# Three edits in a fused transformer-layer kernel: decay rows asked for earlier, one product moved from ScalarE to GpSimd, four loads moved to another queue

## The chip, the cores and the metric

One core of a Trainium2 chip runs the whole program. The core has five engines that run side by side, each with an instruction queue of its own that it works through in order: TensorE (PE; weight loads are shown apart as PEld), VectorE (DVE), ScalarE (ACT), GpSimd (POOL) and SyncE (SP), which does no arithmetic and issues transfers. Transfers can be issued from SP's, ACT's and POOL's queues. The metric is the device time of one launch in microseconds (us).

## The reference

One layer of a streaming encoder works on 576 tokens (a prompt of 512 and a second sequence of 64), with 1024 channels in float32:

```python
def layer(x, lp, st):
    h = x + 0.5 * swiglu(rmsnorm(x, lp['norm_ffn1']), lp['w_ffn1_in'], lp['w_ffn1_out'])
    mix, new_st = mixer(rmsnorm(h, lp['norm_mix']), lp, st)
    h = h + mix
    h = h + 0.5 * swiglu(rmsnorm(h, lp['norm_ffn2']), lp['w_ffn2_in'], lp['w_ffn2_out'])
    return h, new_st
```

The mixer projects its input once and feeds three branches: a state-space scan (SSD: 16 heads in 4 groups), attention over a band of chunks (8 heads), and a matrix memory (mLSTM: 4 heads). In the two scans a running sum of decays along the tokens is used three ways:

```python
# SSD, one chunk
cum = jnp.cumsum(dtc * a, axis=1)
seg = cum[:, :, None] - cum[:, None, :]
lmat = jnp.exp(jnp.where(causal, seg, -jnp.inf))
w = cb[..., None] * lmat * dtc[:, None]
y = jnp.einsum('btsgr,bsgrp->btgrp', w, xc)
y = y + jnp.exp(cum)[..., None] * jnp.einsum('btgn,bgrpn->btgrp', cc, h)
last = cum[:, -1]
wd = jnp.exp(last[:, None] - cum) * dtc
h = jnp.exp(last)[..., None, None] * h + jnp.einsum('bsgr,bsgn,bsgrp->bgrpn', wd, bc, xc)
```

The three branches are normed, projected, weighted by gates (a sigmoid of part of the same projection), summed and projected once more.

## The kernel before

Tokens lie along the free dimension in five chunks (`CH`: four of 128 and one of 64), channels on the 128 partitions. A float32 product is made of three TensorE products of rounded parts: each weight block is split into `ph` (a cast on ACT, L288) and `pl` (the difference, on DVE, L289), and so are the inputs. Weights come through rings of buffers: SP's queue loads `wr` and `wx` blocks from DRAM (L237, L460, L467), POOL adds some of them (an accumulating transfer at L461, sums `wy` and `wx` at L472), ACT and DVE make the parts. Large products use seven block products in place of eight (`stream`, `product`, L616); their results lie in PSUM accumulators that ACT (L533, L540) or DVE (L542) must read out before TensorE can fill them again.

In the mixer the projection runs as one long sequence of such block products (`pairs`), and the small work of the branches is threaded into it. Each branch unit is a Python generator: `attn(i)`, `ml(h)`, `ssd(g)`. `product` calls `tick` once, ahead of its twelve matmuls; `tick` advances `side` (the generator `gates`, which makes decay sums from the gate rows at the start of the stage) and the first unit of `jobs`. A `yield n` in a unit means that its next part is emitted n products later. Units are queued in the order `ORDER` (a0 a1 m0 s0 a2 a3 s1 m1 s2 m2 s3 m3), each when its projections have been emitted. What is emitted is then ordered on each engine by a planner that simulates time: it goes by the order of emission, with `high_priority` and `issue_after` to move it, and issues ahead what is ready.

The running sums per head lie as single rows in a DRAM scratch (`scr`, 24 rows: 0 to 15 SSD's, 16 to 19 and 20 to 23 mLSTM's). `gates` writes them with three stores on SP (L839, L853, L856). A unit reads them back spread over 128 partitions: `rows(r0, n, step)` is an access pattern with partition stride 0, one or two rows wide. They land in `R1`, a tile of eight rows of 576 that holds the residual at other times: rows 0 and 1 hold SSD's gate z, rows 2 to 4 and 5 to 7 are two slots, handed out in turn by `b` to each mLSTM unit and each half of an SSD unit (a unit `ssd(g)` has two halves j = 0, 1 of two heads). All these loads are issued from ACT's queue, L181 and L1175, at the start of the unit that uses them.

In `ssd`, per half: from the spread rows come `wd` (DVE L1209, L1210, then ACT L1214) and `el` (ACT L1212, L1213); x is transposed by TensorE, and DVE writes it scaled by dt into `xd` (L1219, L1223). ACT makes `xw` = `xd` x `wd`, one instruction per chunk and head (L1228). The spread rows themselves become the decay matrix in place (ACT L1234 per chunk, L1236, L1237; POOL L1238, L1239). TensorE then makes the state products from `xw` (L1252) and the outputs (L1274, L1281). The result goes by POOL (L1283 to L1287) to the DRAM scratch `ys`.

`attn` loads its bias (ACT's queue, L916) into one of two buffers `bias` and prepares it on POOL (L918 to L921); DVE adds it to the scores (L965, L980, L981).

After the last unit, `merge` reads the branch outputs `ys` back (tile `y`, L1340), splits them into `YH`, `YL`, and multiplies. Its first four loads, attention's, are issued from SP's queue with raised priority, the others and the gates (L1354) from POOL's.

Of the kernel before, what the change touches and what calls it, by code (L numbers as in the profile page):

```python
# [27 lines left out]
AF = mybir.ActivationFunctionType  # L28
ALU = mybir.AluOpType
AX = mybir.AxisListType  # L30

T = 576
TP = 512
HALVES = ((0, 256), (256, 320))
CH = [(0, 128), (128, 128), (256, 128), (384, 128), (512, 64)]
# [1 line left out]
NS = 115  # L37
FH = 288
NPLAIN = 4
BUFS = {"g": 9, "t": 5, "P": 4, "Q": 2, "bias": 2}  # L40

FBUFS = {"P": 5, "g": 5, "s": 3}
WBUFS = {"wr": 5, "wx": 4, "wy": 2, "ph": 6, "pl": 6}
# [38 lines left out]
class Hybrid:  # L82
    def __init__(self, ctx, tc, I, O):
        self.tc, self.nc, self.I, self.O = tc, tc.nc, I, O
        self.op = None
        self.stay = {}
        self.plan = []
        self.splan = []
        self.ahead = {}
        self.pin = {}  # L90
        self.b_i = 0
        self.jobs, self.gap, self.side = deque(), 0, iter(())
        nc = self.nc
        self.const = ctx.enter_context(tc.tile_pool(name="const", bufs=1))
        self.dram = ctx.enter_context(tc.tile_pool(name="scr", bufs=1, space=bass.MemoryType.DRAM))
        c = self.const
        self.R1 = c.tile([128, 8, T], F32, name="R1")
        self.rs = c.tile([128, T], F32, name="rs")
        self.small = ctx.enter_context(tc.tile_pool(name="small", bufs=8, reuse_waits="tile"))

        self.wt = ctx.enter_context(tc.tile_pool(name="wt", bufs=1, reuse_waits="tile"))
        self.xs = self.dram.tile([128, 8, T], F32, name="xs")

        self.ys = [self.dram.tile([128, T], F32, name=f"ys{i}") for i in range(16)]
        self.gs = [self.dram.tile([128, T], F32, name=f"gs{i}") for i in range(24)]
        self.scr = self.dram.tile([24, T], F32, name="scr_rows")
# [55 lines left out]
    def t(self, tag, shape=(128, T)):  # L162
        pool = self.gp if tag == "g" else self.fp
        return pool.tile(list(shape), F32, name=tag, tag=tag, bufs=BUFS[tag])

    def P(self, shape=(128, T)):
        pool, bufs = (self.fp, BUFS["P"]) if self.mixer else (self.wp, FBUFS["P"])
        return pool.tile(list(shape), F32, name="P", tag="P", bufs=bufs)

    def Q(self, shape=(128, 5, 128)):  # L170
        return self.fp.tile(list(shape), F32, name="Q", tag="Q", bufs=BUFS["Q"])

    def unit(self, shape, tag, bufs):
        return self.fp.tile(list(shape), F32, name=tag, tag=tag, bufs=bufs)

    def b(self, step, r0):


        i = 2 + self.b_i % 2 * 3
        self.b_i += 1  # L180
        self.nc.scalar.dma_start(self.R1[:, i:i + 2, :], self.rows(r0, 128, step))  # L181
        return [self.R1[:, i + j, :] for j in range(3)]

    def bank(self):
        i = self.bank_i % self.banks
# [598 lines left out]
    def gates(self, pre):  # L784
# [3 lines left out]
        nc, TM = self.nc, self.TM  # L788
        view = lambda i, w: self.R1[:, i, 0:5 * w].rearrange("p (c w) -> p c w", w=w)
        X, u, d, p, q = view(1, 24), view(2, 20), view(3, 20), view(4, 20), view(5, 20)  # L790
        nc.gpsimd.memset(X[64:128, 4, :], 0.0)
        ps = self.ps("x")
        for c, (a, n) in enumerate(CH):
            nc.tensor.transpose(ps[:n, c * 24:(c + 1) * 24], pre[0:24, a:a + n], self.ident[0:24, 0:24])
# [34 lines left out]
        nc.vector.tensor_tensor(TM[:, :, 64:68], X[:, :, 20:24], TM[:, :, 96:100], op=ALU.subtract)  # L829
        yield  # L830
        RT, b, g, M, ei = (self.R1[:, i, :] for i in (6, 2, 3, 4, 5))
        ps, ps2 = self.ps("x"), self.ps("s")
        for c, (a, n) in enumerate(CH):
            o = ps[:, a:a + n] if c < 4 else ps2[:, 0:n]
            nc.tensor.transpose(o, TM[:n, c, :], self.ident[:n, :n])
        for dst, r, m in ((b, 96, 4), (g, 64, 4), (RT, 32, 16)):
            nc.scalar.copy(dst[0:m, 0:512], ps[r:r + m, :])
            nc.scalar.copy(dst[0:m, 512:576], ps2[r:r + m, 0:64])
# [28 lines left out]
            nc.tensor.transpose(ps[:n, c * 4:c * 4 + 4], b[0:4, a:a + n], self.ident[0:4, 0:4])  # L867
        nc.vector.tensor_copy(TM[:, 0:4, 96:100], ps[:, 0:16].rearrange("p (c w) -> p c w", w=4))
        nc.vector.tensor_copy(TM[:64, 4, 96:100], ps[:64, 16:20])

    def rows(self, r0, n, step=0):

        return bass.AP(self.scr.tensor, self.scr.offset + r0 * T, [[0, n]] + [[step * T, 2]] * bool(step) + [[1, T]])
# [158 lines left out]
    def ml(self, h, t):  # L1032
        nc = self.nc
        q, k, v, o = t["q"], t["k"], t["v"], t["o"]
        nmB, eiB, _ = self.b(4, 16 + h)
        C0 = self.unit([128, 130], "c0", 1)
        nc.scalar.dma_start(C0[:, :129], self.I["mc0"][h])
        kt, v1 = self.t("t", (128, 5, 128)), self.t("t", (128, 5, 129))
# [17 lines left out]
        s = self.ps("s")  # L1056
# [15 lines left out]
        for c, (a, n) in enumerate(CH):  # L1072
            if c == 4:
                C = C0
            wv = self.unit([128, 130], "wv", 2)
            nc.scalar.activation(wv[:n, :129], v1[:n, c, :], AF.Copy, scale=wc[:n, c:c + 1])
            pc = self.ps("s")
            nc.tensor.matmul(pc[:, :129], kt[:n, c, :], wv[:n, :129], start=True, stop=True)
            C2 = self.unit([128, 130], "cs", 4)
            if c == 0:  # L1080
                nc.vector.tensor_copy(C2[:, :129], pc[:, :129])
            else:
                nc.vector.scalar_tensor_tensor(C2[:, :129], C[:, :129], eiB[:, a + n - 1:a + n], pc[:, :129],
                                               op0=ALU.mult, op1=ALU.add)
            b, o0 = where[c]
            ps = nums[b][:n, o0:o0 + 129]
            nc.tensor.matmul(ps, D[:n, a:a + n], v1[:n, c, :], start=True, stop=(c == 0))
            if c:
                nc.tensor.matmul(ps, qt[:, a:a + n], C[:, :129], start=False, stop=True)
            C = C2  # L1090
            if c >= 3:
                nc.sync.dma_start(self.O["c"][c - 3, h], C[:, :129])
            yield 1
        r = self.unit([128, 8], "r", 2)
        ss = self.unit([128, 8], "ss", 2)
# [2 lines left out]
        for c, (a, n) in enumerate(CH):  # L1098
            b, o0 = where[c]
# [3 lines left out]
        for c, (a, n) in enumerate(CH):  # L1103
            b, o0 = where[c]
# [6 lines left out]
        for c, (a, n) in enumerate(CH):  # L1111
            b, o0 = where[c]
# [55 lines left out]
    def ssd(self, g, t):  # L1168
        nc = self.nc
        Bf, Cf = t["B"], t["C"]  # L1170
        rows = []
        for j in range(2):
            rows.append(self.b(1, 4 * g + 2 * j))
            for r in range(2):
                nc.scalar.dma_start(rows[j][2][r * 64:(r + 1) * 64, :], self.rows(4 * g + 2 * j + r, 64))  # L1175

        last = nc.scalar.activation(self.R1[:, 0, :], self.R1[:, 0, :], AF.Silu)
        with self.tc.issue_after(last.ins):
# [3 lines left out]
        h4 = lambda ap: ap.rearrange("p c (h e) -> p c h e", e=64)  # L1182
# [4 lines left out]
        for c in range(4):  # L1187
# [3 lines left out]
                                op=ALU.mult)  # L1191
# [7 lines left out]
        for j in range(2):  # L1199
# [4 lines left out]
            wd = self.unit([128, 5, 2], "wd", 2)  # L1204
            el = self.unit([128, 5, 2], "el", 2)
            nc.gpsimd.memset(wd[:, 4, :], 0.0)
            for r in range(2):
# [3 lines left out]
                                        op=ALU.subtract)  # L1211
# [3 lines left out]
            xd, xw = self.t("t", (128, 5, 128)), self.t("t", (128, 5, 128))  # L1215
            ps = self.ps("x")
            for c in range(4):
# [4 lines left out]
            nc.tensor.transpose(ps[:64, :128], x[:, 515:579], self.ident)  # L1222
            nc.vector.tensor_tensor(h4(xd[:64, 4:5, :]), ps[:64, :128].rearrange("p (c h e) -> p c h e", h=2, e=64),  # L1223
                                    self.TM[:64, 4:5, d0:d0 + 2].unsqueeze(3).broadcast_to([64, 1, 2, 64]), op=ALU.mult)
            for c, (a, n) in enumerate(CH):
                for r in range(2):
                    hs = slice(r * 64, (r + 1) * 64)
                    nc.scalar.activation(xw[:n, c, hs], xd[:n, c, hs], AF.Copy, scale=wd[:n, c, r:r + 1])  # L1228

            for r in range(2):  # L1230
                e = cum[r]
                tc_ = 32 + d0 + r
                for c, (a, n) in enumerate(CH):
                    nc.scalar.activation(e[:n, a:a + n], e[:n, a:a + n], AF.Relu, scale=-1.0,  # L1234
                                         bias=self.TM[:n, c, tc_:tc_ + 1])
# [10 lines left out]
            for c, (a, n) in enumerate(CH):  # L1246
# [9 lines left out]
                else:  # L1256
                    h = states[c]
                    for r in range(2):
                        hs = slice(r * 64, (r + 1) * 64)
# [9 lines left out]
            for c, (a, n) in enumerate(CH):  # L1269
                if c == 4:  # L1270
                    ps = self.ps("s")
                for r in range(2):
                    o = py[r * 64:(r + 1) * 64, a:a + n] if c < 4 else ps[r * 64:(r + 1) * 64, 0:64]
# [13 lines left out]
            nc.gpsimd.tensor_tensor(R[:, 512:], x[:, 515:], R[:, 512:], op=ALU.mult)  # L1287
            nc.sync.dma_start(self.ys[8 + 2 * g + j], R)
            yield 1
        yield 3  # L1290

        for j in range(2):
# [35 lines left out]
    def merge(self):  # L1328
        nc, tc = self.nc, self.tc
# [8 lines left out]
        def load(src, eng=nc.gpsimd):  # L1338
            y = ys.pop() if ys else self.mp.tile([128, T], F32, name="y", tag="y", bufs=4)
            eng.dma_start(y, src)  # L1340
            return y
# [5 lines left out]
        def fill(n):  # L1347
            while gates and len(loaded) < n:
                i = gates.popleft()
                if i in STAY:  # L1350
                    y = self.stay[i]
                else:
                    y = self.t("g")
                    self.last = nc.gpsimd.dma_start(y, self.gs[i]).ins  # L1354
                loaded.append((i, y))
# [17 lines left out]
        def heads(*which, eng=nc.gpsimd):  # L1373
            for i in which:
                y = load(self.ys[i], eng)
                if i < 4:
                    self.split(y, YH[:, i, :], YL[:, i, :])
                else:
                    self.scaled(y, C_ML - 4, YH, YL, i, slice(0, T), tile=True)
# [13 lines left out]
                self.split(y, ZH[:, k, :], ZL[:, k, :])  # L1393

        with tc.high_priority(offset=1500):
            heads(0, 1, 2, 3, eng=nc.sync)
        fill(5)
        half(1, (0, 1))
        heads(4, 5, 6)
        half(1, (2, 3))  # L1400
        heads(7)
        ssd(range(2))
        half(2, (0, 1))
        ssd(range(2, 5))
        half(2, (2, 3))
        ssd(range(5, 8))
        tiles = [(("w_proj_ssd", 0, 1024, n * 128, 128), [(0, put(n, 0))]) for n in range(8)]
        self.gemm(tiles[:4], ZH, ZL)
# [200 lines left out]
```

## Time and profile before

| | |
|---|---|
| median of 3 runs | 1942.54 us (1939.22, 1942.54, 1944.31) |
| profiled execution, its own time | 1944.79 us |
| its span, first to last instruction | 1943.1 us, 37678 instructions |
| mean granted TensorE clock | 0.991 |
| the mixer's branches up to the start of the merge | about 623 to 1217 us of the span |

The profile is of one execution. "Busy" is the time in which an engine ran instructions other than waits, branches and transfer issues. A group's row gives the source line, the engine, the operation, what it writes and reads (`out<-in`), shapes, count, then busy time and mean ns of one, then the engine's idle time before them and who ended most of it. In a row of the timeline stand start, duration, engine, line, and in brackets the idle time before it with its releaser. A row of stretches gives PE, PEld, DVE, ACT and POOL busy time in turn, then the granted TensorE clock (1.00 is full), the share of transfer engines busy, and GB/s.

### The profile page before, as it was taken

What the parts mean: (1) busy time and instruction counts of PE and PEld (TensorE: products, weight loads), DVE (VectorE), ACT (ScalarE), POOL (GpSimd) and SP (SyncE); (2) the same over time, 40 slices, a digit from 0 to 9 for tenths busy, and PEclk for the clock granted to TensorE, in tenths of its full rate; (3) what the DMA queues carried; (4) which work ended last, traced back from release to release, by engine and by line L of the source; (5) the groups of instructions that cost most, each with busy time, mean ns of one, the idle gap of its engine ahead of it and who ended that gap; (6) DMA issues with size and microseconds to landing.
All of it is one profiled execution on the core that took longest, in us unless ns stands there. A gap on an engine that the chain in (4) does not pass through costs nothing. (4 is left out here: it accounts for less than half of the span.)

```text
span 1943.1 us, 37678 instructions
## 1 busy us (share of the span) xinstructions
PE 1887.2 (97%) x13901; PEld 1823.6 (94%) x13901; DVE 1524.6 (78%) x2715; ACT 1089.5 (56%) x2486; POOL 680.1 (35%) x656
## 2 busy tenths in 40 slices
PE   9999999999999999999999998999999999999998
PEld 8899999999999878888888888999999999999998
DVE  8998998988768767667777775745898888988865
ACT  4554654655544777767675765324555455554544
POOL 5343333333202234323435353440233334334311
PEclk9999999999999999899999999999999999999999
DMA  7267666666742545753667557742236666666631
GB/s 241 74 160 173 159 163 163 159 172 163 185 131 80 156 117 159 200 147 108 183 165 183 155 152 213 241 143 88 77 99 165 163 157 172 166 157 167 159 94 60
DMA packets 129440, 294.69 MB, mean 152 GB/s; under 512 B 14289, under 2 KB 26193, under 8 KB 129257
## 3 DMA queue, kind: packets, MB, share of 16 engines
q1 hardware_dynamic: 100072, 205.67, 32.7%
q0 software_dynamic: 19696, 72.10, 20.5%
q10 hardware_dynamic: 9488, 14.53, 2.6%
q8 instruction: 109, 1.79, 0.4%
q14 instruction: 75, 0.61, 0.1%
HBM read 272.87 MB, written 19.38 MB: 150 GB/s over the span
## 5 line engine op out<-in xcount | busy, mean ns | idle before, releaser
L616 PE MATMUL acc<-TH,ph 128*128 128x288 f32 x3220 | 968.0, 301 | 27.4 <-ACT uv L533 11.8
L616 PE MATMUL acc<-TL,ph 128*128 128x288 f32 x3220 | 955.4, 297 | 0.6 <-DVE TL L289 0.6
L616 PE MATMUL acc<-TH,pl 128*128 128x288 f32 x3220 | 955.0, 298 | 1.0 <-DVE pl L289 0.9
L616 PEld LDWEIGHTS acc<-TH,ph 128*128 128x128 f32 x3220 | 607.5, 189 | 46.9 <-ACT uv L533 15.5
L616 PEld LDWEIGHTS acc<-TL,ph 128*128 128x128 f32 x3220 | 609.4, 189 | 4.9 <-issue 3.7
L616 PEld LDWEIGHTS acc<-TH,pl 128*128 128x128 f32 x3220 | 608.4, 189 | 4.8 <-DVE pl L289 2.2
L289 DVE TENSOR_TENSOR pl<-wr,ph 128x512 fp32r<-128x512 f32 x471 | 429.4, 919 | 76.9 <-ACT ph L288 64.5
L288 ACT CAST ph<-wr 128x512 fp32r<-128x512 f32 x471 | 287.9, 620 | 267.9 <-PE acc L616 141.3
L289 DVE TENSOR_TENSOR pl<-wx,ph 128x512 fp32r<-128x512 f32 x390 | 328.1, 845 | 44.5 <-ACT ph L288 37.9
L288 ACT CAST ph<-wx 128x512 fp32r<-128x512 f32 x390 | 237.4, 621 | 201.3 <-POOL wx L472 110.2
L472 POOL TENSOR_TENSOR wx<-wx,wr 128x512 f32<-128x512 f32 x160 | 246.3, 1539 | 188.2 <-DVE pl L289 150.4
L461 POOL DMA_DIRECT2D wx<-in_sblk x115 | 101.6, 901 | 524.1 <-DMA wx<-in_sblk 154.7
L260 PE MATMUL acc<-YH,ph 128*128 128x256 f32 (+1 forms) x768 | 226.5, 298 | 6.3 <-ACT YH L288 5.8
L260 PE MATMUL acc<-YL,ph 128*128 128x320 f32 (+1 forms) x768 | 227.1, 297 | 2.3 <-DVE YL L339 1.9
L260 PE MATMUL acc<-YH,pl 128*128 128x256 f32 (+1 forms) x768 | 226.5, 296 | 0.1
L260 PEld LDWEIGHTS acc<-YH,ph 128*128 128x128 f32 x768 | 145.4, 190 | 6.9 <-ACT YH L288 5.9
L260 PEld LDWEIGHTS acc<-YL,ph 128*128 128x128 f32 x768 | 145.4, 189 | 3.5 <-DVE YL L339 3.3
L260 PEld LDWEIGHTS acc<-YH,pl 128*128 128x128 f32 x768 | 145.2, 189 | 0.3 <-DVE pl L289 0.3
L472 POOL TENSOR_TENSOR wy<-wx,wr 128x512 f32<-128x512 f32 x35 | 56.2, 1605 | 136.0 <-DVE pl L289 120.0
L655 DVE SCALAR_TENSOR_TENSOR R<-acc,R 128x288 f32<-128x288 f32 x168 | 75.7, 450 | 18.6 <-PE acc L616 18.1
L288 ACT CAST TH<-g 128x288 fp32r<-128x288 f32 x120 | 51.6, 434 | 59.8 <-POOL g L641 34.6
L289 DVE TENSOR_TENSOR pl<-wy,ph 128x512 fp32r<-128x512 f32 x70 | 59.8, 857 | 29.6 <-ACT ph L288 26.6
(320 smaller groups left out, 2393.4 us busy)
## 6 DMA issues: line engine op xcount, KB each, us to landing
wr<-in_sblk SPq DMA_DIRECT2D x345, 256.0 KB, 3.6
wx<-in_sblk SPq DMA_DIRECT2D x115, 512.0 KB, 3.8
wx<-in_sblk POOLq DMA_DIRECT2D x115, 512.0 KB, 6.8
wr<-in_wblk SPq DMA_DIRECT2D x126, 256.0 KB, 3.0
R<-scr_rows ACTq DMA_DIRECT2D x12, 576.0 KB, 5.9
gs<-g SPq DMA_DIRECT2D x20, 288.0 KB, 4.5
g<-gs POOLq DMA_DIRECT2D x20, 288.0 KB, 3.9
y<-ys POOLq DMA_DIRECT2D x12, 288.0 KB, 3.8
```

The source lines that it names most:

```text
L260: nc.tensor.matmul(ps[:, :n], wt[:, wsl], xx[:, k0 + k, a:a + n], start=(k == 0 and i == 0), stop=(k == nk - 1 and i == 2))
L288: self.nc.scalar.copy(hi, src)
L289: self.nc.vector.tensor_tensor(lo, src, hi.bitcast(F32), op=ALU.subtract)
L461: return {"x12": x12, "src": src}, lambda: nc.gpsimd.dma_start(x12, src[:, 1:3, :], accum_op=ALU.add)
L472: add = lambda o, one, two: self.nc.gpsimd.tensor_tensor(o, one, two, op=ALU.add)
L616: self.nc.tensor.matmul(ps, wt[:, wsl], xx[:, kk, :], start=(start and kk == 0 and i == 0), stop=(kk == 3 and i == 2), skip_group_check=True)
L655: self.nc.vector.scalar_tensor_tensor(o, ps, scale, o, op0=ALU.mult, op1=ALU.add)
```

## The change

- `rows_m(h)` and `rows_s(g, j)` take the place of `b`. They issue the spread-row loads from SP's queue: the first ones at the end of `gates`; those of `ml(h + 1)` in `ml(h)` after its last chunk; those of half j of `ssd(g + 1)` at the end of half j of `ssd(g)`. mLSTM's rows get a tile `rm` of their own; SSD's halves have a fixed slot of `R1` each.
- `bias` has one buffer in place of two.
- `xw` is made by two POOL instructions with `wd` broadcast along the head's channels (one for the four full chunks, one for the last), in place of ten on ACT.
- `gates` yields once before its first transposes.
- `merge` issues attention's four output loads from ACT's queue.

```diff
-BUFS = {"g": 9, "t": 5, "P": 4, "Q": 2, "bias": 2}
+BUFS = {"g": 9, "t": 5, "P": 4, "Q": 2, "bias": 1}
...
-    def b(self, step, r0):
-        i = 2 + self.b_i % 2 * 3
-        self.b_i += 1
-        self.nc.scalar.dma_start(self.R1[:, i:i + 2, :], self.rows(r0, 128, step))
-        return [self.R1[:, i + j, :] for j in range(3)]
+    def rows_m(self, h):
+        o = self.unit([128, 2, T], "rm", 1)
+        self.nc.sync.dma_start(o, self.rows(16 + h, 128, 4))
+        self.ahead["m", h] = [o[:, j, :] for j in range(2)]
+
+    def rows_s(self, g, j):
+        nc, i, r0 = self.nc, 2 + 3 * j, 4 * g + 2 * j
+        nc.sync.dma_start(self.R1[:, i:i + 2, :], self.rows(r0, 128, 1))
+        for r in range(2):
+            nc.sync.dma_start(self.R1[r * 64:(r + 1) * 64, i + 2, :], self.rows(r0 + r, 64))
+        self.ahead["s", g, j] = [self.R1[:, i + k, :] for k in range(3)]
...
         nc.gpsimd.memset(X[64:128, 4, :], 0.0)
+        yield
         ps = self.ps("x")
...
         nc.vector.tensor_copy(TM[:64, 4, 96:100], ps[:64, 16:20])
+        self.rows_m(0)
+        for j in range(2):
+            self.rows_s(0, j)
...
-        nmB, eiB, _ = self.b(4, 16 + h)
+        nmB, eiB = self.ahead.pop(("m", h))
...
                 nc.sync.dma_start(self.O["c"][c - 3, h], C[:, :129])
+            if c == 4 and h < 3:
+                self.rows_m(h + 1)
             yield 1
...
-        rows = []
-        for j in range(2):
-            rows.append(self.b(1, 4 * g + 2 * j))
-            for r in range(2):
-                nc.scalar.dma_start(rows[j][2][r * 64:(r + 1) * 64, :], self.rows(4 * g + 2 * j + r, 64))
+        rows = [self.ahead.pop(("s", g, j)) for j in range(2)]
...
-            for c, (a, n) in enumerate(CH):
-                for r in range(2):
-                    hs = slice(r * 64, (r + 1) * 64)
-                    nc.scalar.activation(xw[:n, c, hs], xd[:n, c, hs], AF.Copy, scale=wd[:n, c, r:r + 1])
+            for n, cs in ((128, slice(0, 4)), (64, slice(4, 5))):
+                nc.gpsimd.tensor_tensor(h4(xw[:n, cs, :]), h4(xd[:n, cs, :]),
+                                        wd[:n, cs, :].unsqueeze(3).broadcast_to([n, cs.stop - cs.start, 2, 64]), op=ALU.mult)
...
             nc.sync.dma_start(self.ys[8 + 2 * g + j], R)
             yield 1
+            if g < 3:
+                self.rows_s(g + 1, j)
         yield 3
...
-            heads(0, 1, 2, 3, eng=nc.sync)
+            heads(0, 1, 2, 3, eng=nc.scalar)
```

More of the change, by code (lines that the diff above doesn't have):

```diff
@@ L90, in __init__ @@
         self.pin = {}
-        self.b_i = 0
         self.jobs, self.gap, self.side = deque(), 0, iter(())
```

## The prediction

> **What bounds the kernel now.** I read the busy shares of the page first, then the stretches, then the waits inside the stretch that the change touches.
>
> ```profile
> span 1943.1 us, 37678 instructions
> PE 1887.2 (97%) x13901; PEld 1823.6 (94%) x13901; DVE 1524.6 (78%) x2715; ACT 1089.5 (56%) x2486; POOL 680.1 (35%) x656
> ```
>
> TensorE is the bound: 97% of the span. A change on other engines can only take back time in which TensorE stands still or runs at a lower granted clock. All edits lie in the mixer's branches and the start of its merge, so one stretch matters (columns: stretch, its length, then PE, PEld, DVE, ACT, POOL busy, granted clock, DMA share, GB/s):
>
> ```profile
> 623.00:1217.00 594.00, 559.47 (x4036) 505.90 (x4036) 415.97 (x882) 409.29 (x1112) 225.62 (x233) 0.98 0.60 161
> ```
>
> Here TensorE idles 594.00 - 559.47 = 34.5 us, and the clock of 0.98 takes some 12 more (594 x 0.02). That is all there is to win. POOL is busy 226 of 594 us: it has room on average. The waits of that stretch (who waited for whom: us in total, times, longest):
>
> ```profile
> POOL wx L461 <- DMA wx<-in_sblk: 79.7, 13, 13.7
> ...
> DVE wd L1209 <- DMA R<-scr_rows: 13.1, 6, 4.0
> ...
> ACT el L1212 <- DMA R<-scr_rows: 11.2, 5, 3.1
> PE acc L616 <- ACT uv L533: 10.9, 10, 2.9
> ...
> PE acc L616 <- DVE pl L289: 0.3, 1, 0.3
> ```
>
> TensorE waits for ACT to read out an accumulator (or, as below, for DVE), and both of them stand, in order, behind waits for the broadcast rows R. One instance shows the link:
>
> ```profile
> 790.17 0.49 DVE L1209 TENSOR_TENSOR wd<-R,TM 128x4 f32<-128x4 f32 x1 [3.96 <-DMA R<-scr_rows]
> ```
> ```profile
> 791.96 0.40 PE L616 MATMUL acc<-TH,ph 128*128 128x288 f32 x1 [1.59 <-DVE g L542]
> ```
>
> DVE stood 3.96 us for the rows; the read-out L542 was queued behind; TensorE lost 1.59 us.
>
> **The change part by part.**
>
> *Rows ahead.* Today a unit issues its row loads when it starts, and again for its second half:
>
> ```profile
> R<-scr_rows ACTq DMA_DIRECT2D x12, 576.0 KB, 5.9
> ...
> bias<-in_bias ACTq DMA_DIRECT2D x4, 256.0 KB, 5.5
> ...
> y<-ys SPq DMA_DIRECT2D x4, 288.0 KB, 8.9
> ```
>
> 5.9 us pass from issue to landing. After the change the same bytes are asked for by the unit before (SSD's by the same half of the group before, mLSTM's into a tile of its own), tens of microseconds early, so the waits above end. I took six stretches that each begin at such a wait and end when the backlog is gone:
>
> ```profile
> 1089.00:1100.00 11.00, 7.50 (x55) 6.99 (x54) 8.85 (x22) 8.01 (x28) 3.13 (x3) 1.00 0.67 171
> ...
> sum 58.00, PE 45.11 PEld 40.59 DVE 36.94 ACT 44.77 POOL 19.78; mean PE 7.52 PEld 6.77 DVE 6.16 ACT 7.46 POOL 3.30
> ```
>
> They lose 58.00 - 45.11 = 12.9 us of TensorE, 3.5 of it in the one shown. Part of it is not the wait but the burst of ACT work that follows (L1234: five steps per row and two rows, in one go once they land). With the rows early that burst is next in line; the scheduler can spread it but not remove it. I take two thirds: -8.6 us (ends -4 and -12.9).
>
> *The clock behind those stalls.* Four stretches ran at half clock:
>
> ```profile
> 793.40:803.70 10.30, 10.30 (x44) 9.31 (x43) 8.48 (x17) 6.20 (x18) 4.56 (x5) 0.50 0.81 224
> 1100.60:1104.00 3.40, 3.40 (x16) 3.40 (x16) 3.03 (x5) 1.47 (x6) 1.45 (x1) 0.50 0.07 20
> 626.20:629.70 3.50, 3.50 (x17) 3.00 (x16) 3.50 (x9) 1.19 (x3) 0.00 (x0) 0.52 0.19 63
> 1213.30:1220.20 6.90, 3.71 (x16) 3.71 (x17) 3.01 (x4) 2.69 (x4) 1.66 (x3) 0.51 0.88 312
> ```
>
> The first two follow the stall at 790 and the stretch that ends at 1100. Half of 10.30 + 3.40 is 6.9 us. The later part of the first may come from its short score matmuls as well, so I count 5.1 (half of the first and last 3.4 us, and half of what is left between): -5.1 us (ends 0 and -6.9). Against this stands the Trainium skill, "TensorE: Matmul & The Clock Gate", Part 1, What's actually happening: the array goes cold after at least one idle window of about 3.4 us. The trace disagrees: 1.59 us idle was enough at 790. By that rule these short stalls cost no clock, and the sum would be the one of the clock rival below.
>
> *Gates one tick later.* The added `yield` puts the transposes of the gate rows behind the first product. Today TensorE waits for their source:
>
> ```profile
> 623.00:627.00 4.00, 1.64 (x11) 1.49 (x11) 4.00 (x9) 1.66 (x4) 0.35 (x2) 0.90 0.22 68
> 766.00:772.00 6.00, 4.87 (x38) 3.83 (x37) 4.01 (x6) 4.19 (x15) 5.87 (x10) 1.00 0.47 141
> 1199.00:1217.00 18.00, 10.85 (x72) 9.71 (x73) 7.13 (x16) 6.11 (x13) 6.14 (x9) 0.90 0.98 292
> ```
>
> 2.4 us are idle in the first of these, and 1.75 follow by the half clock at 626. DVE is busy for all four of the 4.00, and the first product needs operands that DVE makes there too, so some of the wait stays: -3.0 us (ends 0 and -4.1).
>
> *SSD's weighted inputs off ACT.* Removed, then the nearest POOL rows for what is added:
>
> ```profile
> L1228 ACT ACTIVATE t<-t,wd 128x64 f32<-128x64 f32 (+1 forms) x80 | 20.7, 339 | 9.9 <-DVE t L1219 8.1 <-DMA st<-in_s 1.8
> ```
> ```profile
> L1238 POOL TENSOR_TENSOR R<-R,t 128x512 f32<-128x512 f32 x16 | 25.7, 1635 | 13.0 <-DVE t L1190 13.0
> ```
> ```profile
> L1287 POOL TENSOR_TENSOR R<-g,R 128x64 f32<-128x64 f32 x8 | 5.2, 654 | 0.0
> ```
>
> ACT loses 20.7 us of work in eight bursts of ten; one of them made the idle 6.00 - 4.87 = 1.1 us of the stretch at 766. I take -0.8 (ends 0 and -1.1). POOL gains 8 x (1.64 + 0.65) = 18.3 us. On the path it counts where the state products L1252 wait for it. Around 1040:
>
> ```profile
> 1038.67 0.68 DVE L1219 TENSOR_TENSOR t<-ps_x,TM 128x512 f32<-128x512 f32 x1
> ```
> ```profile
> 1041.00 0.99 POOL L1287 TENSOR_TENSOR R<-g,R 128x64 f32<-128x64 f32 x1
> ```
> ```profile
> 1043.20 0.60 PE L1252 MATMUL ps_s<-t 128*128 128x128 f32 x4
> ```
>
> The scaled inputs are there at 1039.35, POOL is busy with the half before until 1041.99, and 2.29 more give 1044.28: 1.1 us after TensorE used them. Only second halves meet that backlog, four of them: 4 x 1.1 = 4.4 us, less what the schedule reorders: +3 (ends 0 and the whole 18.3). No gain is possible by this alone, since TensorE does not wait for POOL here today. DVE is slowed beside POOL:
>
> ```profile
> 760.54 0.69 DVE L289 TENSOR_TENSOR pl<-wr,ph 128x512 fp32r<-128x512 f32 x1
> ```
> ```profile
> 763.69 3.48 DVE L289 TENSOR_TENSOR pl<-wr,ph 128x512 fp32r<-128x512 f32 x2
> ```
>
> Alone 0.69, beside L1238 1.74 each: 8 x 1.05 = 8.4 us more DVE work, under DVE's 178 idle us of the stretch, so nothing on the path. The Trainium skill, "SBUF — State Buffer", section SBUF: two separate sides, has it harsher: one of the two engines takes the shared ports for a whole instruction and the other fully blocks. By that DVE would lose up to 18.3 us, still under its cover; the trace shows a slowdown of 1.05, not a block.
>
> *Merge's first loads on ACT's queue.* The four loads take 8.9 us each, issued from SP at
>
> ```profile
> 1207.57 2.08 SPq L1340 DMA_DIRECT2D y<-ys  x4
> ```
>
> TensorE idles 18.00 - 10.85 = 7.15 us in the stretch from 1199, most of it until they land, and loses 1.85 more by half of the 3.71 busy at half clock from 1213. The DMA share is 0.98 there, so another queue helps only if the loads are asked for earlier than 1207.57, and the profile does not show when their tiles came free. -1.5 us (ends +1, ACT held by a load that waits for its tile, and -9.0).
>
> *SP's queue and the bias buffer.* 28 row loads move to SP: the 12 of the row above and 16 narrow ones (two per half in the code). Weight loads queue behind them. A row load of the next group waits for the readers of the old rows, which the store just ahead of it waits for as well. Only the first rows wait anew, for three small stores to land. The cover is the ring of weights: TensorE waited 0.3 us in all for a weight's `pl` in this stretch. If that cover is gone, each late load is a stall of TensorE. 0 (ends 0 and +4). With one bias buffer, a unit's bias is loaded only after the last use by the one before:
>
> ```profile
> 679.20 0.24 DVE L981 TENSOR_TENSOR ps_s<-ps_s,bias 64x64 f32<-64x64 f32 x1
> ```
> ```profile
> 688.60 0.50 DVE L965 TENSOR_TENSOR ps_s<-ps_s,bias 128x128 f32<-128x128 f32 x2
> ```
>
> 9.4 us lie between; the load takes 5.5, which leaves 3.9 for POOL's preparation of it: 0 (ends 0 and +2).
>
> *New order.* Queues are ordered by a planner that simulates time, so every queue of the stretch is dealt anew, and stalls of the kind above fall elsewhere. The stalls of this stretch that none of the edits touches are 34.5 - 12.9 - 2.4 - 1.1 - 7.15 = 11 us; I take a quarter more of them, +3 (ends -3 and +8).
>
> **Sum.** -8.6 - 5.1 - 3.0 - 0.8 + 3 - 1.5 + 0 + 3 = -13.0 us against the span of 1943.1, or 1944.79 for the profiled execution, which lies 2.25 above the median of 1942.54. 1942.54 - 13.0 = 1929.5; I say **1930 us**, its own range 1922 to 1938.
>
> **Rivals.** *Stalls only move (no change).* The row waits go, ACT's bursts and the new order give the same back, the clock drops elsewhere. For it: ACT and DVE are both busy about 70% of the stretch. Against it: the waits hold both at once, and 12.9 us follow them closely. Gates and merge alone stay: about -3, 1939.
>
> *POOL becomes late (slower).* POOL works in order and stands for landing weights 79.7/13 = 6.1 us a time. Caught behind one, the weighted inputs come 6.1 + 2.3 - 3.85 (from 1039.35 to 1043.20) = 4.5 us late. Without the POOL term the sum is -16.0, so it decides from 16.0/8 = 2.0 us late per half on average. Six of eight caught give 27 - 16 = +11: 1954.
>
> *Everything goes.* All terms at their lower ends, half of the merge: -12.9 - 6.9 - 4.1 - 1.1 - 4.5 = -29.5, with +3 for POOL -26.5: 1916.
>
> *The clock does not follow.* Cold stretches come from the short score matmuls and not from the stalls. Then 5.1 and the 1.75 at the gates stay: 1930 + 6.8 = 1937. This is the time by the clock page's rule, which the row at 793 contradicts.
>
> **How the numbers follow.** Forecast 0.45, stalls move 0.17, POOL late 0.13, everything 0.15, clock 0.10. 0.3% is 5.8 us, about what a measurement of this kernel can tell from no change: faster means under 1936.7. Forecast, everything and half of the clock case are faster: 0.65; stalls move and the other half, 0.22; POOL late, 0.13. The range runs from 1918 (most of "everything") to 1944 (all of "stalls move"), leaving out about 0.2.
>
> **What would show it.** Right: no DVE or ACT wait on rows longer than 1 us, granted clock near 1.00 from 780 to 820 and 1100 to 1120, first transposes of the gates after the first product, TensorE idle under 22 us in the mixer's stretch. Wrong: TensorE or its weight loads waiting for the POOL product at the state products, SP's weight loads landing late with TensorE waiting for `pl`, or ACT standing at a merge load. The prediction falls if idle of TensorE does not drop, or if it drops and the clock's share does not rise.

## Result: slower by 0.9%, and the profile after

The changed kernel takes 1958.88 us (median of 4 runs, 1953.77 to 1961.36) against 1940.88 beside it: a ratio of 1.0092, 95% interval 1.0074 to 1.011. The forecast was 1930 (range 1918 to 1944), so the sign was wrong. The profiled execution of the change took 1953.77, the fastest of its four. The head of its page, its mixer stretch and the waits on rows there:

```profile
span 1952.1 us, 37615 instructions
PE 1888.8 (97%) x13901; PEld 1828.8 (94%) x13901; DVE 1541.3 (79%) x2715; ACT 1067.2 (55%) x2404; POOL 702.9 (36%) x672
```
```profile
626.00:1226.00 600.00, 557.33 (x4029) 507.66 (x4028) 423.69 (x880) 388.34 (x1029) 248.06 (x247) 0.97 0.58 158
```
```profile
PE acc L622 <- ACT uv L539: 16.5, 10, 4.0
...
DVE wd L1217 <- DMA R<-scr_rows: 14.2, 7, 3.8
...
ACT L1220 <- DMA R<-scr_rows: 8.9, 3, 3.9
...
ACT wc L1077 <- DMA rm<-scr_rows: 8.3, 3, 5.8
...
ACT el L1220 <- DMA R<-scr_rows: 6.5, 3, 2.7
```

TensorE idles 600.00 - 557.33 = 42.7 us in the stretch, against 34.5 before, and the clock there is 0.97 against 0.98. ACT's load moved as worked out, 409.29 to 388.34 (-21); POOL's moved a little more than the 18.3 worked out, 225.62 to 248.06 (+22). The waits on rows, which were to end, are all there: 14.2 + 8.9 + 8.3 + 6.5 = 37.9 us in these four rows, and 40.2 with two small ones, against 39.4 in the kernel before. One of them, from issue to damage:

```profile
745.32 0.38 SPq L178 DMA_DIRECT2D rm<-scr_rows  x1
```
```profile
754.29 1.04 ACT L1077 ACTIVATE wc<-TM,rm 128x1 f32<-128x1 f32 x5 [5.82 <-DMA rm<-scr_rows]
755.23 0.60 ACT L294 CAST ph<-wr 128x512 fp32r<-128x512 f32 x1
```
```profile
755.87 0.69 DVE L295 TENSOR_TENSOR pl<-wr,ph 128x512 fp32r<-128x512 f32 x1 [6.49 <-ACT ph L294]
```
```profile
756.93 0.48 PE L1131 MATMUL ps_x<-ident,Q 128*128 128x128 f32 x1 [4.85 <-DVE Q L1125]
```
```profile
756.40:759.80 3.40, 2.87 (x12) 2.87 (x13) 2.38 (x9) 3.37 (x6) 0.98 (x1) 0.50 0.27 84
```

The rows for the *next* mLSTM unit are asked for at 745.32. ACT reaches `wc`, the first reader, 3.15 us later (754.29 - 5.82 = 748.47); the load lands 8.9 us after its issue. ACT stands 5.82 us, the weight split behind `wc` is late, so DVE stands 6.49 and TensorE 4.85, and the next 3.4 us run at half clock. Nothing needed `wc` yet. The next step that reads it ran from 977.7 on:

```profile
L1086 ACT ACTIVATE wv<-t,wc x5: 398/399/407, 977.7 to 986.1; 128x129 f32<-128x129 f32 x4, 64x129 f32<-64x129 f32 x1
```

Here the reader had been put right behind the load, far ahead of its use.

This could have been seen in the trace of before:

```profile
L181 ACTq DMA_DIRECT2D R<-scr_rows x2: 333/333/333, 952.4 to 981.2; - x2
```
```profile
L1212 ACT ACTIVATE el<-R x4: 194/202/212, 957.6 to 987.5; 128x4 f32<-128x4 f32 x4
```
```profile
L1177 ACT ACTIVATE R<-R x1: 688/688/688, 1013.8 to 1013.8; 128x576 f32<-128x576 f32 x1
```

The columns are, as in the row above, count, shortest/median/longest ns, first and last start. The third row is the first step of the third SSD unit, at 1013.8. Its row loads ran at 952.4 and 981.2, up to 61 us ahead of it, and `el`, which reads them, at 957.6 and 987.5, some 5 to 6 us behind each. The second SSD unit is further apart still: its first step on ACT is at 907.2, its row loads ran at 781.0 and 796.7, up to 126 us ahead. So in the kernel before, too, the loads were issued long before their unit, and each reader stood a few us behind its load.

### The profile page after: what moved, and what is told of

It is laid out like the page before. It is cut to its first block, busy times and chain, and to the rows that moved or that the text cites. A ratio compares the mean times of both kernels' runs of the same rounds, so it can differ in the third digit from the quotient of the medians.

```text
span 1952.1 us, 37615 instructions
## 1 busy us (share of the span) xinstructions
PE 1888.8 (97%) x13901; PEld 1828.8 (94%) x13901; DVE 1541.3 (79%) x2715; ACT 1067.2 (55%) x2404; POOL 702.9 (36%) x672
## 3 DMA queue, kind: packets, MB, share of 16 engines
q0 software_dynamic: 19696, 72.10, 20.3%
## 5 line engine op out<-in xcount | busy, mean ns | idle before, releaser
L295 DVE TENSOR_TENSOR pl<-wr,ph 128x512 fp32r<-128x512 f32 x471 | 443.9, 950 | 78.0 <-ACT ph L294 65.2
L295 DVE TENSOR_TENSOR pl<-wx,ph 128x512 fp32r<-128x512 f32 x390 | 321.6, 829 | 29.4 <-ACT ph L294 22.2
L266 PE MATMUL acc<-YL,ph 128*128 128x256 f32 (+1 forms) x768 | 228.5, 299 | 2.5 <-DVE YL L345 1.9
```

What stands on the lines that cost most here:

```text
L266: nc.tensor.matmul(ps[:, :n], wt[:, wsl], xx[:, k0 + k, a:a + n], start=(k == 0 and i == 0), stop=(k == nk - 1 and i == 2))
L295: self.nc.vector.tensor_tensor(lo, src, hi.bitcast(F32), op=ALU.subtract)
```

## What the runs lose, and where

Each run has a span and a mean granted clock. Span x clock is the time at full speed, span x (1 - clock) the time lost to half clock (medians over the runs of a kernel):

| kernel | runs | ratio to before, 95% interval | at full speed | lost to the clock |
|---|---|---|---|---|
| before | 23 | 1 | 1922.6 | 13.6 |
| the change | 4 | 1.0092 (1.0074 to 1.011) | 1924.1 | 31.3 |
| rows ahead alone | 6 | 1.0059 (1.0037 to 1.008) | 1921.9 | 26.3 |
| weighted inputs on POOL alone | 6 | 1.0043 (1.002 to 1.0067) | 1921.0 | 25.3 |
| merge's loads on ACT alone | 11 | 1.0003 (0.9991 to 1.0016) | 1922.8 | 15.5 |
| gates one tick later alone | 11 | 1.0019 (1.0005 to 1.0034) | 1924.6 | 15.6 |

The 23 runs of before are those beside the four parts; in the other sets of runs before lost 13.6 or 15.5 us. The clock is recorded to 0.001 of its full value, which is 1.9 us of such a span.

Between before and the change the time at full speed differs by 1.5 us and the loss to the clock by 17.7. That is the most that the clock can have cost, since TensorE also stands idle in half-clock time (the prediction's stretch at 1213.30 has 3.71 us busy in 6.90). In the two profiled executions, which differ by 9.0 us, the idle time of the stretch alone rose by 8.2. So stalls and clock both grew, and these columns do not part one from the other.

The clock's own record is made of cells of 3.41 us, each at 1.00 or 0.50. Over the 17 profiles of this case, their first and last 20 us left out, 93 half-clock cells follow a full-clock one. In all 93 TensorE had idled at least 1.22 us in the cell ahead; of the full-clock cells with 1.85 us idle or more, 55 of 55 were followed by a half-clock one; between the two bounds it went either way. So a stall of some 1.8 us within one cell costs up to 1.7 us on top of itself (an estimate: half of a cell of 3.41 us at half clock, if TensorE is busy throughout), and two stalls of 0.9 us in different cells cost only themselves. TensorE's stalls of 1.6 us or more in the mixer: 4 before, 9 with rows ahead alone, 10 with the weighted inputs alone, 7 with the whole change. That count does not order the kernels by itself either: the whole change has fewer such stalls than two of its parts and is slower than both.

The Trainium skill, "TensorE: Matmul & The Clock Gate", Part 1, What's actually happening, has the array go cold after at least one idle window of about 3.4 us. The window's length agrees with the cells of 3.41 us. Read as a window that is idle throughout, the rule does not agree, since 1.85 us within a cell were always enough.

## The experiments

**One part at a time, on the kernel before.** The theories: A, readers hoisted behind their loads; B, POOL's product late; C, every new order costs a few us.

```diff
# rows ahead: rows_m, rows_s, tile rm, bias in one buffer; nothing else of the change
-        nmB, eiB, _ = self.b(4, 16 + h)
+        nmB, eiB = self.ahead.pop(("m", h))
# weighted inputs
-                    nc.scalar.activation(xw[:n, c, hs], xd[:n, c, hs], AF.Copy, scale=wd[:n, c, r:r + 1])
+                nc.gpsimd.tensor_tensor(h4(xw[:n, cs, :]), h4(xd[:n, cs, :]), wd[...broadcast...], op=ALU.mult)
# merge
-            heads(0, 1, 2, 3, eng=nc.sync)
+            heads(0, 1, 2, 3, eng=nc.scalar)
# gates
+        yield
```

> The kernel before with the rows part alone (rows_m and rows_s on SP's queue, tile rm, one bias buffer); the rest as before. Theory A (the first users of the rows are planned right behind the load, wherever the load is put, and SP's loads land later than ACT's did): slower by 6 to 16 us, with DVE, ACT still waiting for rows 25 us or more in total, single waits up to 6 us. Theory B (the loss comes from the POOL product): faster by 5 to 10 us, row waits near nothing. Theory C (no part carries it, every new order of the queues costs a few us): slower by 0 to 5, and the other three parts likewise.

> The kernel before with SSD's weighted inputs on GpSimd alone. Theory A: within 4 us of before, either way. Theory B: slower by 8 to 18 us, with TensorE or its weight loads waiting on the POOL product at the state products. Theory C: slower by 0 to 5.

> The kernel before with the merge's first four loads on ACT's queue alone. Theories A and B: within 3 us of before; the loads are asked for no earlier than in before, since they are planned at the same time. Theory C: slower by 0 to 5. If the 5.8 us stall at the merge's start is the loads' queue, faster by 3 to 6.

> The kernel before with the added yield in gates alone. Theories A and B: faster by 2 to 4 us, the 2.4 us of TensorE ahead of the gates' transposes gone and full clock after it. Theory C: slower by 0 to 5 in spite of it.

Measured beside before at 1938.17: rows 1950.65, weighted inputs 1948.32, merge 1938.53, gates 1943.58. No part gains. Rows ahead, groups of the first readers (busy, mean ns, then idle before them):

```profile
L1076 ACT ACTIVATE wc<-TM,rm 128x1 f32<-128x1 f32 (+1 forms) x20 | 4.2, 282 | 10.0 <-DMA rm<-scr_rows 10.0
L1216 DVE TENSOR_TENSOR wd<-R,TM 128x4 f32<-128x4 f32 x16 | 3.6, 234 | 11.9 <-DMA R<-scr_rows 11.7 <-POOL t L1048 0.2
L1219 ACT ACTIVATE el<-R 128x4 f32<-128x4 f32 x16 | 3.2, 200 | 5.1 <-DMA R<-scr_rows 5.1
```

The readers still wait 27 us, now in bigger pieces on ACT (`wc` up to 5.1 a time). Two timeline rows of TensorE in the same kernel, both ended by a read-out on ACT, and the row of ACT just ahead of the first read-out:

```profile
941.18 0.40 PE L622 MATMUL acc<-TH,ph 128*128 128x288 f32 x1 [2.26 <-ACT g L546]
959.40 0.40 PE L622 MATMUL acc<-TH,ph 128*128 128x288 f32 x1 [3.30 <-ACT g L546]
```
```profile
937.92 2.92 ACT L1241 ACTIVATE R<-R,TM 128x128 f32<-128x128 f32 x10
```

Ahead of 941.18 ACT had not waited for rows for 9 us: they had landed, and it was busy with ten decay steps on them. Ahead of 959.40 it had waited 1.76 us for rows until 953.61 and then worked through ten such steps as well. So a reader that is put too early costs in two ways: its engine stands until the rows land, or it works on them in front of a read-out that TensorE needs.

The weighted inputs alone show waits on rows again, 46.5 us in all against 39.4 in before, and not a late POOL. Waits on rows in that kernel, and one instance:

```profile
DVE wd L1209 <- DMA R<-scr_rows: 13.0, 6, 3.3
DVE P L1049 <- DMA R<-scr_rows: 13.0, 3, 6.0
...
ACT wc L1067 <- DMA R<-scr_rows: 8.7, 3, 3.8
...
ACT R L1241 <- DMA R<-scr_rows: 7.9, 4, 4.1
```
```profile
1042.04 0.29 ACT L1067 ACTIVATE wc<-TM,R 128x1 f32<-128x1 f32 x1 [3.81 <-DMA R<-scr_rows]
```
```profile
1044.32 0.40 PE L616 MATMUL acc<-TH,ph 128*128 128x288 f32 x1 [3.27 <-ACT uv L533]
```

With 20 us of work taken off, ACT reached this reader 4.0 us after its load was issued (at 1034.2), where in before it was 6.4 us; the load took 7.9. TensorE's 3.27 us stand behind ACT's 3.81. This is one instance; the runs with held readers below test it. TensorE never waits for the POOL product itself, here or in the change; ACT does once, 2.0 us. Theory A's numbers were missed in two of the four: it had the weighted inputs within 4 us of before and the gates 2 to 4 us faster; by their ratios they are 8 and 4 us slower.

The gates' stall went (from 2.37 us to under 0.7 in that kernel). The first merge product waited 7.3 us there in place of 5.8; whether the one led to the other is not shown.

```profile
PE acc L260 <- ACT YH L288: 7.3, 1, 7.3
```

**Holding the readers.** The next kernels keep every load as it is and forbid the first readers, and SSD's decay steps on the rows, to stand ahead of their own unit's start on their engine (main lines of the edit):

```diff
+    @contextmanager
+    def held(self, *ins):
+        with ExitStack() as es:
+            for i in ins:
+                es.enter_context(self.tc.issue_after(i))
+            yield
...
-            nc.scalar.activation(wc[:n, c:c + 1], ...)
+            with self.held(hk[0]):      # ACT's copy of the unit's first turned operand; D on DVE likewise
+                nc.scalar.activation(wc[:n, c:c + 1], ...)
...
+            with self.held(ha, hv):     # the unit's first silu (ACT), the product cb (DVE)
                 nc.vector.tensor_tensor(wd[:, 0:4, r], last, ...)
                 nc.scalar.activation(el[:, 0:4, r], last, AF.Exp)
```

It was put on the kernel before, on rows ahead, and on the whole change. A fourth kernel is rows ahead without hold, its loads on ACT's queue, to tell the queue apart from the hoisting.

> The kernel before, with one thing added: the first readers of the rows (SSD's wd, el, and the steps on the rows; mLSTM's wc and D) may not be put ahead of their own unit's start on their engine. Theory A (the planner puts each reader 2 to 5 us behind its load, however long before it is needed, and the load lands later than planned): the waits of ACT and DVE on rows, 39.4 us in the profile of before (20.0 + 19.4), fall under 10, half-clock time in the mixer's stretch falls from 27 us to under 17, and the time is 1926 to 1933 against 1938. Theory C (every new order costs some us, whatever waits go): the waits fall too, but the time is 1940 to 1950.

> Rows ahead on SP's queue (the part alone, 1950.7) with the same hold on the first readers. Theory A: with no reader hoisted behind its load, it does not matter that SP's loads take longer; waits on rows under 8 us, time within 4 us of the held kernel before (1926 to 1936), so the part costs nothing by itself. If SP's queue is the trouble (row loads delay the weight loads there): waits go, but 1944 to 1952 stays. Theory C: 1945 to 1955.

> The whole change with the same hold on the first readers. Theory A, in which also the loss of the weighted-inputs part comes from readers of rows that arrive too early: 1928 to 1940 against 1958.9 for the change as it is. Theory B (the POOL product itself is late or slows others): 8 us above the held rows kernel. Theory C: 1950 to 1962.

> Rows ahead as in the part alone, but their loads issued on ScalarE's queue as before, no hold. Theory A: the readers are hoisted behind the loads there too, so waits on rows stay above 20 us and the time is 1944 to 1954; the shorter landing on this queue (5.9 us against 6 to 9) gives back 5 us at most. If SP's queue is the trouble: 1936 to 1942.

Beside before at 1939.08: before held 1932.77 (ratio 0.9965, 0.9952 to 0.9978), rows ahead held 1930.53 (0.9958, 0.9944 to 0.9973), the whole change held 1940.52 (1.001, 0.9998 to 1.0021), rows ahead on ACT's queue 1961.18 (1.0117, 1.0095 to 1.0138). The same groups of readers in rows ahead held, and its mixer stretch:

```profile
L1086 ACT ACTIVATE wc<-TM,rm 128x1 f32<-128x1 f32 (+1 forms) x20 | 4.2, 289 | 0.0
L1231 ACT ACTIVATE el<-R 128x4 f32<-128x4 f32 x16 | 3.2, 202 | 0.0
...
L1228 DVE TENSOR_TENSOR wd<-R,TM 128x4 f32<-128x4 f32 x16 | 2.7, 174 | 0.0
```
```profile
625.20:1201.30 576.10, 549.89 (x4033) 500.36 (x4033) 412.73 (x882) 409.67 (x1111) 227.26 (x233) 0.99 0.61 164
```

With the readers held, rows ahead goes from 0.59% above before to 0.42% below, and the stretch is 576.1 us long against 600.0 in the change. For this part theory A is shown: with the loads coded as they were and only the readers moved, its whole loss goes. C is not the rule, since these kernels too have a new order. On the kernel before the hold alone gains 0.35%: idle in the stretch falls from 34.5 to 25.0 us. Held against held, rows ahead and before differ by 0.07% with overlapping intervals, so no run shows that asking for the rows earlier gains anything by itself.

Two things are not shown. First, the hold moves the decay steps as well (on ACT they start at 679.3 to 1066.7 us in rows ahead, at 757.2 to 1129.7 with the hold), so these runs do not part the waits from the work put too early. The waits alone do not order the kernels: 39.4 us before, 28.2 with rows ahead alone, and only 23.6 in the fourth kernel, the slowest of all. Second, the whole change held is at 1940.52, just outside theory A's 1928 to 1940 and 10 us above rows ahead held, a step of the size that theory B gave. Held against held it is still 0.45% slower than before (1.001 against 0.9965), about half of its loss. The section after this looks for that rest.

On the clock, in the profile of before held the half-clock time counted there did not fall (27.3 us in both, 13.7 of them now at the merge), so that number of the expectation was missed. By span and clock the held kernels lost no less to the clock than before did beside them: 20.3 us (before held) and 17.4 (rows ahead held) against 15.5. Their gain is all in the other column, 1911.3 and 1911.9 us against 1922.3.

SP's queue was not the trouble: with the same loads on ACT's queue the kernel is 1.17% above before, on SP's 0.59%. The first of these is slower than either theory had it, and why is open. The readers still wait (first row), and in its profile one stall of 1.58 us is followed by 20.5 us at half clock (second row):

```profile
ACT wc L1076 <- DMA rm<-scr_rows: 11.4, 4, 4.4
```
```profile
694.90:715.40 20.50, 19.86 (x49) 9.81 (x50) 8.00 (x21) 12.22 (x36) 1.27 (x1) 0.50 0.01 2
```

**Building the held change up again.** The steps from rows ahead held (1930.53) to the whole change held (1940.52), the weighted inputs on the held kernel before, and the bias buffer alone; the edits are those of the diff above, singly or together.

> Rows ahead with held readers (1930.5) plus the merge's first loads on ScalarE's queue. Theory A: the loads are asked for no earlier, so 1928 to 1934. Theory C (each new order costs some us): 1934 to 1940.

> The kernel of the run above plus the gates one tick later: rows held, merge loads and yield, the weighted inputs still on ScalarE. Theory A: the 2.4 us stall at the gates goes and some of it comes back later, as when the yield stood alone (1943.6 against 1938.2): 1928 to 1936. If the weighted inputs are all that parts this kernel from the whole held change, it is 1930 to 1934 and the whole one 1940.5; if the yield carries part of that, 1934 to 1938.

> The kernel before with held readers (1932.8) and the weighted inputs on GpSimd, nothing else. Theory A (alone it cost 8 to 10 us because ACT, lighter by 20 us of work, was put in front of row loads sooner): with no such waits left 1930 to 1936. Theory B (POOL is late, by itself or by what queues behind it there): 1938 to 1944, with TensorE waiting 1 to 2 us at the products that read POOL's masked rows.

> The kernel before with one buffer instead of two for attention's bias, nothing else. By the prediction it costs nothing: 1936 to 1941 against about 1938.5. If POOL's 6 to 8 us waits for the bias load reach TensorE: 1942 to 1948, with TensorE stalls over 1.5 us in the attention units (660 to 740 and 820 to 900 us).

Beside before at 1940.2: rows and merge 1931.19 (0.9956), and the yield 1932.02 (0.996), weighted inputs on before held 1934.34 (0.9969), one bias buffer 1940.25 (1.0007, 0.9996 to 1.0018). So merge and yield show no cost clear of the intervals there, and neither does the bias buffer. The weighted inputs lose 0.0004 of the held ratio, where without hold they lost 0.0043. In the held kernel TensorE does wait for POOL a little:

```profile
PE ps_v L1287 <- POOL R L1250: 4.7, 3, 1.9
```

That is not POOL's new product but the masked rows of the decay matrix that follow it on POOL. Theory B has a part in these 4.7 us only.

> Rows ahead with held readers (1930.5) and the weighted inputs on GpSimd. If the weighted inputs cost about 1 us once the readers are held, as on the kernel before: 1930 to 1934, and the rest comes with yield or merge. If GpSimd's product meets the rows on SP's queue badly: 1937 to 1943, with TensorE waiting 4 to 8 us for GpSimd's masked rows and for read-outs by ACT.

> The kernel of the run above and the gates one tick later; the merge's first loads still on SP's queue. If the yield makes the difference: 1937 to 1943 while the run above stays at 1930 to 1934. If the merge's loads behind ACT's longer work do: 1930 to 1935 here too, and only the whole held change is at 1940.

> The change as it is (1958.9), without hold, with the weighted inputs back on ScalarE. If their loss adds up as in the single parts (+8 to +10): 1948 to 1953. If the rows' hoisted readers alone carry the loss and ACT's 20 us make no odds beside them: 1955 to 1961.

Beside before at 1938.07: rows and weighted inputs held 1938.94 (1.0004), with the yield 1941.25 (1.0013), the change without hold but the weighted inputs back on ACT 1954.55 (1.0079, 1.0065 to 1.0092). The weighted inputs thus cost 0.1% in the unheld change (the two intervals overlap), but 0.46% on rows ahead held. The last kernel lies between the two ranges given for it, so the parts neither add up nor leave ACT's 20 us without effect. Against rows ahead held the first of these has 33.0 us idle in the mixer instead of 26.2: 4.4 at the merge's first product (2.5 in the other), 3.4 for POOL's masked rows (2.0 for ACT's weighted inputs in the other), and the rest in read-outs. Its time is the one given for the second case of its expectation, and POOL's masked rows and the read-outs have a part in it. No single wait carries it; why the two parts, harmless singly once held, cost 8 us together stays open.

## Why the prediction was wrong, point by point

*Rows ahead, -8.6, and the clock behind it, -5.1: the step that failed.* It rested on "Today a unit issues its row loads when it starts", as the code reads. The trace of before had them up to 126 us ahead of the unit, and the wait was made by where the planner puts the reader. Asking still earlier moved load and reader together, so the waits stayed: 40.2 us against 39.4. The prediction's own sign of right and wrong (no wait on rows over 1 us) failed with 3.8 and 5.8 us in the change. The readers are what has to be moved: with them held, the kernel before gains 0.35%, 6.8 us, against the 13.7 of these two terms, and none of it through the clock; the earlier loads add nothing clear of the noise (0.07%).

*The clock.* That short stalls cost clock, against the rival by which it does not follow, was right: 17.7 us at most of the loss. But it worked the other way, as there were 7 stalls of 1.6 us or more in place of 4. The prediction's list of half-clock stretches also lacks one, 3.41 us from 687.6 on.

*Gates, -3.0.* The stall went (0.31 us in the change); no gain followed. Alone the edit costs 0.19%.

*Weighted inputs, -0.8 and +3.* The work was sized well: POOL's product takes 18.8 us in the change, 2.35 per half against 2.29 worked out, and DVE's busy time rose by 7.7 us (8.4 worked out). The place was wrong: on the kernel before the product costs 0.43%, and 0.04% with the readers held, so there it cost through the readers and not through POOL. On rows ahead held it costs 0.46% by a path that stays open.

```profile
L1234 POOL TENSOR_TENSOR t<-t,wd 128x512 f32<-128x512 f32 (+1 forms) x16 | 18.8, 1194 | 0.1
```

The reading "a slowdown of 1.05, not a block" is not shown by the row at 763.69. POOL's product L1238 took 1.28 us at 920.09, where no DVE work overlapped it, and 1.75 at the median of 16, so both engines were held up, and two engines that shut each other out in turn could give rows of this kind as well.

*Merge's loads, -1.5, and the bias buffer, 0.* Both nothing, as their ranges allowed. In the change the stall at the merge became two waits for POOL, the longer of which stood behind a gate load in its queue:

```profile
1218.32 0.71 PE L336 MATMUL ps_x<-ident,sm 128*128 128x128 f32 x4 [1.53 <-POOL sm L312]
1224.06 1.84 PE L336 MATMUL ps_x<-ident,sm 128*128 128x128 f32 x6 [4.48 <-POOL sm L312]
```
```profile
POOL g L1363 <- DMA ys<-g: 4.4, 1, 4.4
```

*New order, +3 (up to +8).* Too small and of the wrong kind: it was taken as a scatter of untouched stalls, where the place that the planner gave to the readers set the sign. *The rivals:* "stalls only move" named the effect but priced it at no change; "POOL late", the only one on the slower side, was another mechanism. None held that the readers move with their loads.

## What to carry to other kernels

Before a load is moved earlier, look in the trace at how far it already lies ahead of its use and at what its first reader waits for: if the planner sets the reader a few us behind the load wherever the load stands, hold the reader, not the load. Here holding the readers, with the rows ahead on SP's queue, gives 0.42% over the kernel before (0.27% to 0.56%) and is the fastest version together with the one that also has the merge's loads on ACT (0.44%); the hold alone gives 0.35%, and the intervals overlap. Look at the bottleneck engine's stalls by length, since here the long ones were followed by half clock.

## What the runs showed of the hardware

- The clock is granted in cells of 3.41 us at 1.00 or 0.50. A cell with 1.85 us idle or more was followed by a half-clock one in 55 of 55 cases, none followed a cell with under 1.22.
- Being busy does not always bring the clock back. In the stretch at 694.9 TensorE was busy 19.86 of 20.50 us and stayed at 0.50 throughout; it ran mostly attention's products then (8.6 us of scores into 64 partitions, 3.9 and 3.6 of products 128 wide), with twelve of the projection's between them. In the row below, of the kernel before, it was busy for all of 6.80 us at half clock, and 23 of the 27 products there are the projection's; so what keeps the clock down is open.

```profile
796.80:803.60 6.80, 6.80 (x27) 6.30 (x28) 6.26 (x9) 2.79 (x8) 4.56 (x5) 0.50 0.92 256
```

- mLSTM's row load, the same each time, landed 6.3 to 8.9 us after its issue from SP's queue in the change, after 6.6 us (median) in rows ahead alone, and after 6.8 to 9.1 us from ACT's queue. Nothing that plans on one figure for a load is right for all of them.
